# A gated sigmoid on one core: stores of four-row groups and a second load held back

## The chip, the cores and the metric

The kernel runs on one core of a Trainium2 chip. The metric is device time in microseconds for one execution. A smaller number is better. Three runs of the kernel before gave 933.16, 933.18 and 934.11 us; their median is 933.18 us.

## The reference

The input is a matrix of 8192 rows and 8192 columns in float32. The left half of each row is multiplied by the sigmoid of the right half, element by element.

```python
def reference(x):                      # x: (8192, 8192) float32
    a, b = np.split(x, 2, axis=-1)
    return a * (1 / (1 + np.exp(-b)))  # (8192, 4096) float32
```

So 268.4 MB have to be read and 134.2 MB written, and each output element needs one sigmoid and one product.

## The kernel before, in words

SBUF, the on-chip memory, has 128 partitions. A tile is 256 consecutive rows: each partition holds `R = 2` neighbouring rows, which lie in one piece of 64 KiB in HBM. There are 32 tiles. A tile goes through four steps.

- **Load** (`load`, line 46). The SP engine issues one DMA of 128 pieces of 64 KiB into one of two load slots, `x_sb0` and `x_sb1` (line 34). Tile i uses slot i mod 2. The load of tile i waits until the products of tile i - 2 are done, since these read the same slot (line 50).
- **Sigmoid** (line 61). ScalarE (ACT) waits for the tile to land and overwrites the right halves in place. A whole tile is one instruction on 128 x 8192 elements. The first and the last tile are cut into four instructions of 128 x 2048 (`fourths`, line 95).
- **Product** (line 72). VectorE (DVE) multiplies the left halves by the sigmoids and writes the packed result into one of two output buffers, `o_sb0` and `o_sb1`, of 32 KiB a partition (line 35). It waits until the store that last used the buffer has landed, and for the sigmoid. One semaphore for each buffer, `ready`, counts both: a store adds 16, the first sigmoid of a tile adds 1 (lines 62 to 66).
- **Store** (`store`, line 78). ACT's queue issues one DMA of 128 pieces of 32 KiB, which waits for the tile's products. The last tile's store is cut into four DMAs of 128 pieces of 8 KiB, issued from SP's queue.

All orders are written out by hand in `trace` (line 91): each engine takes its instructions in the order in which the loop emits them, and a waiting instruction holds those behind it on its engine. On ACT the order is sigmoid of tile i, store of tile i, sigmoid of tile i + 1. On SP it is one load after the other, then the last stores. The load of tile 0 is moved ahead of the program's start barrier (`_launch_early`). At the end (`close`) GpSimd clears the semaphores, and SP waits for the last stores.

Loads and stores run on the same 16 DMA engines through two queues: q1 is fed by SP, q10 by ACT. In the profile an entry such as "SPq" or "ACTq" is a DMA that the engine issues. Both load slots and both output buffers together take 192 KiB of each partition.

Of the kernel before, what the change touches and what calls it, by code (L numbers as in the profile page):

```python
# [1 line left out]

# [4 lines left out]

P = 128
R = 2
SLOTS = 2  # L10


class _Program:

    def __init__(self, nc, x, out):
        self.nc = nc
        fp32 = mybir.dt.float32
        n_rows, n_cols = x.shape
        self.half = n_cols // 2  # L30
        self.n_tiles = n_rows // (P * R)
        self.x = x.rearrange("(n p r) m -> n p (r m)", p=P, r=R)
        self.out = out.rearrange("(n p r) m -> n p (r m)", p=P, r=R)
        self.xs = [nc.alloc_sbuf_tensor(f"x_sb{s}", [P, R * n_cols], fp32).ap() for s in range(SLOTS)]
        self.os = [nc.alloc_sbuf_tensor(f"o_sb{s}", [P, R * self.half], fp32).ap() for s in range(SLOTS)]
        self.loaded = [nc.alloc_semaphore(f"loaded{s}") for s in range(SLOTS)]
        self.ready = [nc.alloc_semaphore(f"ready{s}") for s in range(SLOTS)]
        self.product = nc.alloc_semaphore("product")
        self.sigmoid = nc.alloc_semaphore("sigmoid")
        self.arrived = nc.alloc_semaphore("arrived")  # L40
        self.last = nc.alloc_semaphore("last")
        self.to_ready = [0] * SLOTS
        self.products = self.sigmoids = self.lasts = 0
        self.done = {}

    def load(self, i, after=None):
        s = i % SLOTS
        ins = self.nc.sync.dma_start(out=self.xs[s][:, :], in_=self.x[i]).then_inc(self.loaded[s], 16)
        if i >= SLOTS:
            ins._wait_ge(self.product, self.done[i - SLOTS])  # L50
        return ins

    def work(self, i, pieces):

        nc, s = self.nc, i % SLOTS
        rows = self.xs[s].rearrange("p (r h m) -> p r h m", r=R, h=2)
        packed = self.os[s].rearrange("p (r m) -> p r m", r=R)
        waits = []
        for k, (r, c) in enumerate(pieces):
            b = rows[:, r, 1, c]  # L60
            sig = nc.scalar.activation(out=b, in_=b, func=mybir.ActivationFunctionType.Sigmoid)  # L61
            if k == 0:
                sig._wait_ge(self.loaded[s], 16 * (i // SLOTS + 1))
                self.to_ready[s] += 1 + (16 if i >= SLOTS else 0)
                waits.append((self.ready[s], self.to_ready[s]))
                sig.then_inc(self.ready[s], 1)
            else:
                self.sigmoids += 1
                waits.append((self.sigmoid, self.sigmoids))
                sig.then_inc(self.sigmoid, 1)  # L70
        for (r, c), wait in zip(pieces, waits):
            mul = nc.vector.tensor_mul(out=packed[:, r, c], in0=rows[:, r, 0, c], in1=rows[:, r, 1, c])  # L72
            mul._wait_ge(*wait)
            mul.then_inc(self.product, 1)
            self.products += 1
        self.done[i] = self.products

    def store(self, i, lo=0, hi=None, products=None):
        s, final = i % SLOTS, i == self.n_tiles - 1
        hi = R * self.half if hi is None else hi  # L80
        queue = self.nc.sync if final else self.nc.scalar
        ins = queue.dma_start(out=self.out[i][:, lo:hi], in_=self.os[s][:, lo:hi])
        ins._wait_ge(self.product, self.done[i] if products is None else products)
        if final:
            self.lasts += 16
            ins.then_inc(self.last, 16)
        else:
            ins.then_inc(self.ready[s], 16)
        return ins

    def trace(self):

        n, half = self.n_tiles, self.half
        whole = [(slice(0, R), slice(0, half))]
        fourths = [(slice(r, r + 1), slice(h * half // 2, (h + 1) * half // 2)) for r in range(R) for h in range(2)]
        self.load(1)
        for i in range(n):
            self.work(i, fourths if i in (0, n - 1) else whole)
            if i + SLOTS < n:
                self.load(i + SLOTS)  # L100
            if i < n - 1:
                self.store(i)
        for k in range(4):
            self.store(n - 1, k * half // 2, (k + 1) * half // 2, self.products - 3 + k)

    def close(self):


        nc, s = self.nc, (self.n_tiles - 2) % SLOTS
        for engine in (nc.scalar, nc.vector, nc.sync):  # L110
            engine.drain().then_inc(self.arrived, 1)  # L111
        nc.gpsimd.wait_ge(self.arrived, 3)
        nc.gpsimd.wait_ge(self.ready[s], self.to_ready[s] + 16)
        ids = sorted(h.num for h in (*self.loaded, *self.ready, self.product, self.sigmoid, self.arrived))
        assert ids == list(range(ids[0], ids[-1] + 1)) and self.last.num not in ids
        nc.gpsimd.sem_clear(range(ids[0], ids[-1] + 1))
        nc.gpsimd.drain()
        nc.sync.wait_ge(self.last, self.lasts).then_inc(self.last, -self.lasts)


def _launch_early(nc):

    SP = mybir.EngineType.SP
    entry, body = (b.instructions for b in nc.main_func.blocks[:2])
    load = next(i for i in body if i.engine == SP and i.opcode == "DMACopy")
    assert not load.sync_info.on_wait
    body.remove(load)
    where = next(k for k, i in enumerate(entry) if i.engine == SP and i.opcode == "Drain")  # L130
    entry.insert(where, load)


@with_exitstack
def kernel(
    ctx: ExitStack,
    tc: tile.TileContext,
    x: bass.AP,
    out: bass.AP,
):  # L140
    nc = tc.nc
    prog = _Program(nc, x, out)
    tc.info.no_tile_sem_insts.add(prog.load(0).ins.name)
    tc.close()
    tc.compile()  # L145
    _launch_early(nc)
    prog.trace()
    prog.close()


# [1 line left out]
_INS = ['x']  # L152
_OUTS = [((8192, 4096), 'float32')]


# [23 lines left out]
```

## Time and profile before

| what | value |
|---|---|
| median of three runs | 933.18 us |
| the profiled execution's own time | 933.08 us |
| its span, first to last instruction | 931.8 us |
| DVE busy, 38 products | 278.6 us |
| ACT busy, 38 sigmoids and a table load | 226.8 us |
| DMA packets, bytes moved | 9649, 402.67 MB |
| mean rate over the span | 432 GB/s |
| DVE waits for ACT | 647.1 us |
| ACT waits for loads | 693.9 us |

Busy times are sums over the span. The span is a little shorter than the execution's time, because something lies before the first and after the last instruction. A wait of a compute engine counts only where it delays the end. The packet count holds the data packets and one small completion packet for each transfer and DMA engine; the latter raises the semaphore by one, so that 16 mean that a transfer has landed.

### The profile page before, as it was taken

How to read it: one execution, taken by the hardware profiler on the slowest of the kernel's cores; microseconds unless marked ns; L12 is line 12 of the kernel's file. 1: busy time of each engine (PE TensorE's matmuls, PEld its weight loads, DVE VectorE, ACT ScalarE, POOL GpSimd, SP SyncE). 2: the span in 40 equal slices, each digit the busy share in tenths (PEclk: the TensorE clock that was granted, in tenths of full speed). 3: DMA queues.
4: the chain of work that ended last, by engine and by line, in shares of the span. 5: the costliest groups of instructions: out<-in, count | busy, mean ns of one | idle time of the engine just before them, and what ended most of it. 6: DMA issues, size and time to landing. Idle time of an engine off the chain costs nothing.

```text
span 931.8 us, 190 instructions
## 1 busy us (share of the span) xinstructions
DVE 278.6 (30%) x38; ACT 226.8 (24%) x39; POOL 0.2 (0%) x4
## 2 busy tenths in 40 slices
DVE  0333213333133331233312333123331233312333
ACT  1323330233311333113331133311333203332033
POOL 0000000000000000000000000000000000000000
DMA  9999999999999999999999999999999999999999
GB/s 405 428 450 428 422 456 405 450 428 428 450 421 435 428 436 442 428 428 450 450 405 430 442 456 428 412 463 408 450 428 428 450 408 447 428 428 450 426 429 405
DMA packets 9649, 402.67 MB, mean 432 GB/s; under 512 B 1072, under 2 KB 1072, under 8 KB 1072
## 3 DMA queue, kind: packets, MB, share of 16 engines
q1 hardware_dynamic: 5184, 272.63, 67.7%
q10 hardware_dynamic: 4464, 130.03, 32.3%
q14 instruction: 1, 0.01, 0.0%
HBM read 268.44 MB, written 134.22 MB: 432 GB/s over the span
## 4 chain that ended last, share of the span: by engine, by line
DMA 73%; DVE 15%; ACT 12%; DVEq 0%; issue 0%
DMA x_sb<-in_x_dram 73%; DVE o_sb L72 15%; ACT x_sb L61 12%; DVEq L111 0%
## 5 line engine op out<-in xcount | busy, mean ns | idle before, releaser
L72 DVE TENSOR_TENSOR o_sb<-x_sb 128x8192 f32<-128x8192 f32 (+1 forms) x38 | 278.6, 7344 | 647.1 <-ACT x_sb L61 647.1
L61 ACT ACTIVATE x_sb<-x_sb 128x8192 f32<-128x8192 f32 (+1 forms) x38 | 225.5, 5949 | 693.9 <-DMA x_sb<-in_x_dram 693.9
L61 ACT ACT_TABLE_LOAD x1 | 1.3, 1283 | 1.4 <-PEq L145 1.4
L163 POOL MEMSET const-bfloat16-1.0<- 128x1 bf16 x1 | 0.1, 102 | 0.0
L163 POOL MEMSET const-uint8-127<- 128x1 uint8 x1 | 0.1, 102 | 0.0
L163 POOL MEMSET const-float32-0.0<- 128x1 f32 x1 | 0.1, 99 | 0.2 <-issue 0.2
L163 POOL MEMSET const-float32-1.0<- 128x1 f32 x1 | 0.1, 99 | 0.0
## 6 DMA issues: line engine op xcount, KB each, us to landing
out_dram<-o_sb ACTq DMA_DIRECT2D x31, 4096.0 KB, 34.8
out_dram<-o_sb SPq DMA_DIRECT2D x4, 1024.0 KB, 5.7
x_sb<-in_x_dram SPq DMA_DIRECT2D x32, 42.2
```

The lines of the kernel that those rows point to most:

```text
L61: sig = nc.scalar.activation(out=b, in_=b, func=mybir.ActivationFunctionType.Sigmoid)
L72: mul = nc.vector.tensor_mul(out=packed[:, r, c], in0=rows[:, r, 0, c], in1=rows[:, r, 1, c])
L163: nc = _bacc.Bacc("TRN2", target_bir_lowering=False, num_devices=1)
```

## The change

Two neighbouring tiles become a group of 512 rows, in which each partition holds four neighbouring rows, 128 KiB in one piece of HBM. A tile is still 64 KiB a partition: tile i is the half i mod 2 of group i div 2. So both the number and the size of the loads stay. In HBM, neighbouring partitions of a load now lie 128 KiB apart instead of 64.

The two output buffers become one of 64 KiB a partition, `o_sb`. The even tile's products fill its first half and the odd tile's its second half, and one store of 128 pieces of 64 KiB writes both, after the odd tile's products. The products of the next even tile wait until the whole store has landed. The SBUF taken is the same.

The loads of even tiles wait as before for the products of the tile that used the slot. The load of an odd tile i + 1 waits on `ready` until the sigmoid of the even tile i has run. `ready` is now a single semaphore: the sigmoid of an even tile adds 32 and a group's store adds 16. For the load the threshold is 16 below the one that the even tile's product waits for, so that the store of the group before need not have landed.

The first tile is cut into two pieces of one row each instead of four. In the last group the even tile is stored by itself with pieces of 32 KiB on ACT's queue, and the odd tile in four quarters as before. GpSimd no longer waits for the last whole-tile store before it clears the semaphores; SP waits for it with the quarters, on `last`.

```diff
-        self.x = x.rearrange("(n p r) m -> n p (r m)", p=P, r=R)
-        self.out = out.rearrange("(n p r) m -> n p (r m)", p=P, r=R)
+        self.x = x.rearrange("(g p r) m -> g p (r m)", p=P, r=2 * R)
+        self.out = out.rearrange("(g p r) m -> g p (r m)", p=P, r=2 * R)
...
-        self.os = [nc.alloc_sbuf_tensor(f"o_sb{s}", [P, R * self.half], fp32).ap() for s in range(SLOTS)]
+        self.os = nc.alloc_sbuf_tensor("o_sb", [P, 2 * self.packed], fp32).ap()
...
-    def load(self, i, after=None):
-        s = i % SLOTS
-        ins = self.nc.sync.dma_start(out=self.xs[s][:, :], in_=self.x[i]).then_inc(self.loaded[s], 16)
-        if i >= SLOTS:
-            ins._wait_ge(self.product, self.done[i - SLOTS])
+    def load(self, i):
+        g, s = divmod(i, 2)
+        part = self.x[g][:, s * self.tile : (s + 1) * self.tile]
+        ins = self.nc.sync.dma_start(out=self.xs[s], in_=part).then_inc(self.loaded[s], 16)
+        if i > 1 and s:
+            ins._wait_ge(self.ready, self.to_ready - 16)
+        elif i > 1:
+            ins._wait_ge(self.product, self.products)
         return ins
...
             if k == 0:
-                sig._wait_ge(self.loaded[s], 16 * (i // SLOTS + 1))
-                self.to_ready[s] += 1 + (16 if i >= SLOTS else 0)
-                waits.append((self.ready[s], self.to_ready[s]))
-                sig.then_inc(self.ready[s], 1)
+                sig._wait_ge(self.loaded[s], 16 * (g + 1))
+            if k == 0 and s == 0:
+                self.to_ready += 32 + (16 if g else 0)
+                waits.append((self.ready, self.to_ready))
+                sig.then_inc(self.ready, 32)
...
-    def store(self, i, lo=0, hi=None, products=None):
-        s, final = i % SLOTS, i == self.n_tiles - 1
-        hi = R * self.half if hi is None else hi
-        queue = self.nc.sync if final else self.nc.scalar
-        ins = queue.dma_start(out=self.out[i][:, lo:hi], in_=self.os[s][:, lo:hi])
-        ins._wait_ge(self.product, self.done[i] if products is None else products)
+    def store(self, g, lo, hi, products, final=False):
+        queue = self.nc.sync if g == self.n_tiles // 2 - 1 and lo else self.nc.scalar
+        ins = queue.dma_start(out=self.out[g][:, lo:hi], in_=self.os[:, lo:hi])
+        ins._wait_ge(self.product, products)
         if final:
             self.lasts += 16
-            ins.then_inc(self.last, 16)
-        else:
-            ins.then_inc(self.ready[s], 16)
-        return ins
+        ins.then_inc(self.last if final else self.ready, 16)
...
         self.load(1)
         for i in range(n):
-            self.work(i, fourths if i in (0, n - 1) else whole)
-            if i + SLOTS < n:
-                self.load(i + SLOTS)
-            if i < n - 1:
-                self.store(i)
-        for k in range(4):
-            self.store(n - 1, k * half // 2, (k + 1) * half // 2, self.products - 3 + k)
+            g, s = divmod(i, 2)
+            self.work(i, by_row if i == 0 else fourths if i == n - 1 else whole)
+            if s == 0 and i > 0:
+                self.load(i + 1)
+            if s == 0 and i < n - 2:
+                self.load(i + 2)
+            if s and i < n - 2:
+                self.store(g, 0, 2 * packed, self.products)
+            elif i == n - 2:
+                self.store(g, 0, packed, self.products, final=True)
+            elif i == n - 1:
+                for k in range(4):
+                    lo = packed + k * half // 2
+                    self.store(g, lo, lo + half // 2, self.products - 3 + k, final=True)
...
-        nc.gpsimd.wait_ge(self.ready[s], self.to_ready[s] + 16)
```

## The prediction

> **What bounds the kernel now.** I read the page's slices first, then its queues and issues, then the instruction groups by shape, the timeline, and last the DMA packets one by one.
>
> ```profile
> span 931.8 us, 190 instructions
> ...
> DVE 278.6 (30%) x38; ACT 226.8 (24%) x39; POOL 0.2 (0%) x4
> ...
> DMA  9999999999999999999999999999999999999999
> ...
> q1 hardware_dynamic: 5184, 272.63, 67.7%
> q10 hardware_dynamic: 4464, 130.03, 32.3%
> ...
> out_dram<-o_sb ACTq DMA_DIRECT2D x31, 4096.0 KB, 34.8
> out_dram<-o_sb SPq DMA_DIRECT2D x4, 1024.0 KB, 5.7
> x_sb<-in_x_dram SPq DMA_DIRECT2D x32, 42.2
> ```
>
> No compute engine passes 30%, the DMA row is 9 in every slice, and the two queues' shares add to 100.0%: all 16 DMA engines work through the whole span. q1 carries loads and the last four stores, q10 the other 31 stores. Only shorter packets can save time, and anything that leaves the DMA engines empty is paid in full. The page's chain, loads 73%, is read accordingly: a load takes 42 us to land because it queues.
>
> ```profile
> L72 DVE TENSOR_TENSOR o_sb<-x_sb 128x8192 f32<-128x8192 f32 x30 | 260.8, 8692 | 608.3 <-ACT x_sb L61 608.3
> L61 ACT ACTIVATE x_sb<-x_sb 128x8192 f32<-128x8192 f32 x30 | 210.9, 7029 | 653.0 <-DMA x_sb<-in_x_dram 653.0
> L72 DVE TENSOR_TENSOR o_sb<-x_sb 128x2048 f32<-128x2048 f32 x8 | 17.8, 2286 | 38.8 <-ACT x_sb L61 38.8
> L61 ACT ACTIVATE x_sb<-x_sb 128x2048 f32<-128x2048 f32 x8 | 14.6, 1898 | 41.0 <-DMA x_sb<-in_x_dram 41.0
> ```
>
> A whole tile costs 7.03 us of sigmoid and 8.69 us of product: 15.7 us, beside 29 us of DMA.
>
> ```profile
> 32.66 57.10 SPq L48 DMA_DIRECT2D x_sb<-in_x_dram  x3
> 32.66 0.38 ACTq L82 DMA_DIRECT2D out_dram<-o_sb  x1
> 44.76 7.03 ACT L61 ACTIVATE x_sb<-x_sb 128x8192 f32<-128x8192 f32 x1 [15.66 <-DMA x_sb<-in_x_dram]
> 51.82 8.69 DVE L72 TENSOR_TENSOR o_sb<-x_sb 128x8192 f32<-128x8192 f32 x1 [19.19 <-ACT x_sb L61]
> 60.55 0.36 ACTq L82 DMA_DIRECT2D out_dram<-o_sb  x1
> ...
> 919.08 6.94 SPq L82 DMA_DIRECT2D out_dram<-o_sb  x4
> ```
>
> From 32.66 us each product releases a load and a store together, so neither queue is empty again before 914 us.
>
> The packet records say the rest. A DMA gives each engine 8 packets and one 4-byte completion packet. A 64 KiB load packet takes 2.418 us, a 32 KiB store packet 1.213, an 8 KiB one 0.309, a completion 0.009. With both queues filled, every engine alternates load and store packets one for one. Loads alone (21 to 33 us) and stores alone (914 to 931 us) keep these durations. The stream runs without a gap from 1.0 us to 931.4 us. The fastest and slowest engine end a transfer 0.5 to 0.7 us apart, and the semaphore follows the slowest by 0.3 to 0.6 us, for a store 0.44 at most.
>
> **The change, part by part.** In what follows E is a group's even tile, O its odd tile.
>
> *Packets.* Thirty 32 KiB-row stores become fifteen 64 KiB-row stores. Per engine 30 x 8 x 1.213 = 291.12 us becomes 15 x 8 packets of 64 KiB. No store of that size is in the trace. Its bounds are two 32 KiB packets (2.426) and the load packet of equal bytes (2.418). I take the load's, whose size it has: 120 x 2.418 = 290.16, so -0.96 us (the other end: 0). Fifteen completions fewer: 15 x 0.009 = -0.14. Loads stay 32 transfers of 128 x 64 KiB.
>
> *First tile in two rows.* Between the shapes' means the sigmoid grows (7029 - 1898) / 6144 = 0.835 ns an element and the product 1.043. Hence 3.61 and 4.42 us for 128x4096. Tile 0 lands at 21.8; two sigmoids and the second product end at 21.8 + 7.2 + 4.4 = 33.4, with starts 33.5. The third load is issued there, while the second has packets until 40.4. Cost nothing, hidden by load 1 with 7 us to spare.
>
> *The cycle.* One group is 24 packets an engine, 8 E, 8 O, 8 store: 58.03 us, if no engine runs dry. I place it from 0 = end of the previous O on the slowest engine, with E queued behind it.
>
> - Semaphore 0.44, sigmoid to 7.50, product to 16.2; store issued. E fills the queue until 19.35. How long until an issued transfer can run? The first load's packets come 1.0 to 1.3 us after issue on idle engines; the last four stores start at most 1.9 us after theirs (919.08, 921.0). So the store is there at 17.2 to 18.1; the fastest engine ends E at 18.65. Margin 0.5 to 1.4 us; it starts at 19.36.
> - E landed at 19.8, sigmoid to 26.85. Only now is O issued (before, the load would have gone out behind the last product, 10 us earlier). The even load behind it on SP is held too, harmless since it waits for a later product anyway. What covers the hold is the store, with the engines to itself until 38.7. The first store of before, issued at 32.66 beside loads, saw two whole load packets end before its own began; packet boundaries up to 3.26 us after issue still went to the other queue. By that row O starts at the boundary after 26.88 + 3.26 = 30.1, at 31.45, behind five store packets. The remaining three store packets alternate with O and the store ends at 19.36 + 11 x 2.418 = 45.96.
> - The product of E waits for that, since the output buffer is single. ACT queues nothing behind it but the sigmoid of O, not yet landed. Semaphore to 46.4, product to 55.1, the next even load available 56.2 to 57.1. O's last packet ends at 58.05, on the fastest engine 57.35. Margin 0.25 to 1.2 us: thin, but positive, so the next group starts in phase. Cost nothing.
>
> [...]
>
> *Tail.* The last product of E frees a 32 KiB-row store of 9.7 us behind the last O. The four quarters of O come 4.2 us after its landing and then every 2.2 us. DMA work left after O is 9.7 + 4 x 2.48 = 19.6 us, and the last quarter is available about 12.7 us after O's end: covered. Before and after end on the same quarter store.
>
> **Sum.** The profiled execution took 933.08 us: span 931.77 and 1.31 around it; the median shown, 933.18, is 0.10 above. 933.08 - 0.96 - 0.14 = **932.0 us**, 0.12% less. A measurement of this kernel can tell about 0.2%, 1.87 us, from no change: this is "same".
>
> **Rivals.**
>
> *Restarts cost (slower).* When the first store woke the empty q10 amid loads, the load packet before it took 3.23 to 3.47 us instead of 2.418 on all engines: 0.92 us in the mean with nothing moved. That happened once, since no queue ran empty again. After, the store queue starts from empty 16 times (15 more) and the load queue 15 times. If each store start costs 0.92: 932.0 + 13.8 = 945.8; if load starts do too: 959.6. Against: q1 ran empty at 914 and woke at 921.0 with no extra time; an instruction fetch on a third queue at 761.6 added 0.24 us beyond its own packet, on one engine. So 0.92 may be the price of a queue's first use. I cost a further restart at 0, the row of the warm queue; bounds 0 and 0.92, or 0.24 (30 x 0.24 = 7.2: 939.2). It decides at (1.87 + 1.10) / 30 = 0.1 us a restart.
>
> *The even load comes late (slower).* If O wakes faster, at 29.03, after four store packets, the store ends at 48.4, and the product and issue reach the engines 1.2 to 2.1 us after the fastest have run dry. Some 1.5 us for each of 15 groups: 954. The row for it is the last stores' 1.9 us; against it the 3.26 above. Even with five packets, half a microsecond beyond the thin margins, once a group, gives 939.5. A store's landing signal 1.56 us later than the 0.44 of the rows would do as much and more, 938 to 952, and I give it 0.03 of the chances below. [...]
>
> *The first restart's price goes too (faster).* If the first store finds only E's last packet, its 0.92 may vanish beside the packet savings: 931.06, just past 0.2%.
>
> *Memory rows.* Partition steps double in HBM, loads 64 to 128 KiB, stores 32 to 64 KiB; every packet could lengthen. The trace shows both old steps at full rate, nothing on the new ones. A 1% longer load packet would give 938.2. [...]
>
> **How the numbers follow.** No stall, 932.0 (931.3 to 935.0): 0.50. Faster, about 931.06: 0.08. Small bubbles (0.24 a restart, half a microsecond a group, a later landing signal with its 0.03, slower rows with 0.02), 935 to 942: 0.17. Store restarts at full price, about 946: 0.12. Both restarts, or the late even load, 950 to 960: 0.13. So faster 0.08, same 0.50, slower 0.42. The range leaves out the last case, the lower part of the fast one and the upper half of the 946 case, together 0.2: 931.0 to 946.5. The likeliest case alone spans 931.3 to 935.0.
>
> **What would show it.** Right: DMA shares still adding to 100%, 64 KiB store packets of 2.418 us, a store landing 30 us after its issue (16.25 to 46.4), an even load 23 us (55.2 to 58.05 + 19.8), an odd one 32 us (26.9 to 58.5), the product of E waiting for the store and not the sigmoid, groups every 58.0 us. Wrong: groups longer than 58.03; load or store packets above 2.43 where a queue starts (restarts); a gap before each even load (late load); all packets longer (memory rows).

## The result and the profile after

The changed kernel takes 961.85 us (median of five runs, 959.98 to 963.74) against 933.2 us before (median of five, 933.16 to 934.11). The ratio is 1.0302, 95% interval 1.029 to 1.0314: about 28.7 us slower. The profiled execution is the one of 961.85 us; its span is 960.5 us against 931.8.

These are the lines of the changed kernel's page that answer to the first fence of the prediction: the span, the compute engines, the DMA engines' busy tenths in 40 slices, the queues (packets, MB, share of 16 engines' span) and the issues (count, KB each, median us from issue to landing).

```profile
span 960.5 us, 186 instructions
...
DVE 278.4 (29%) x36; ACT 226.6 (24%) x37; POOL 0.2 (0%) x4
...
DMA  9999999999999989999999999999999899999999
...
q1 hardware_dynamic: 5184, 272.63, 67.1%
q10 hardware_dynamic: 2304, 130.02, 31.8%
...
out_dram<-o_sb ACTq DMA_DIRECT2D x1, 4096.0 KB, 13.7
out_dram<-o_sb SPq DMA_DIRECT2D x4, 1024.0 KB, 8.6
x_sb<-in_x_dram SPq DMA_DIRECT2D x32, 28.2
out_dram<-o_sb ACTq DMA_DIRECT2D x15, 33.1
```

The compute engines did the same work. The two queue shares show the loss in two parts. They add to 98.9%, where before they added to 100.0%: 0.011 x 960.5 = 10.6 us in which a DMA engine had no packet. And the packets themselves take 0.989 x 960.5 = 949.9 us of engine time, 18 us more than the 931.8 before, although there are fewer of them.

Two lines of the waits and a stretch of the timeline show where. The waits have the waiting engine and line, what it waited for, the total in us, how often, and the longest.

```profile
DVE o_sb L81 <- DMA out_dram<-o_sb: 498.7, 15, 34.2
DVE o_sb L81 <- ACT x_sb L69: 174.4, 17, 26.9
```

```profile
57.06 0.38 ACTq L90 DMA_DIRECT2D out_dram<-o_sb  x1
60.92 7.03 ACT L69 ACTIVATE x_sb<-x_sb 128x8192 f32<-128x8192 f32 x1 [12.62 <-DMA x_sb<-in_x_dram]
67.98 31.59 SPq L53 DMA_DIRECT2D x_sb<-in_x_dram  x2
90.53 8.69 DVE L81 TENSOR_TENSOR o_sb<-x_sb 128x8192 f32<-128x8192 f32 x1 [33.50 <-DMA out_dram<-o_sb]
100.19 7.03 ACT L69 ACTIVATE x_sb<-x_sb 128x8192 f32<-128x8192 f32 x1 [32.24 <-DMA x_sb<-in_x_dram]
```

Every even tile's product waits for the group's store, as forecast. But it starts at 90.53 us and ends at 99.2, and only then is the next even load issued (the second of the two SP issues). The odd load has landed by 100.2 and nothing else is queued. The packet records of one DMA engine over the same stretch, start times in us, say why (E is a group's even tile, O its odd tile, S the store):

```
last load packet of E   57.18, 2.85 us long (2.418 is usual)
store packets           60.04 (3.12 us long)  63.15  65.57  67.98  70.39
O and store alternate   O 72.81  S 75.25  O 77.66  S 80.08  O 82.49  S 84.91
                        O 87.32                  the 8th and last store packet ended at 87.32
store's completion      89.73                    its own turn, after one more load packet
O alone                 89.74  92.15  94.57  96.98, ends 99.40
next even load          101.19                   issued 99.2
```

A packet is called long here when it takes more than the usual time of its size, 2.418 us for 64 KiB and 1.213 for 32 KiB; what is added up is the excess. From the packet records of all 16 engines, in the mean per engine: 10.1 us more than before without a packet; 5.3 us of long first packets of even loads behind such a gap; 14.4 us of long packets where a store starts (last load packet 8.9, first store packet 5.5), of which 0.9 stood in the kernel before; 0.3 us where an odd load starts; and 1.1 us saved by fewer packets. -1.1 + 10.1 + 5.3 + 13.5 + 0.3 = 28.1 of the 28.7 us. Eight of the even loads come late; each leaves the engines empty for 0.2 to 2.3 us in the mean and has a first packet that is 0.6 to 0.7 us too long, about 1.9 us together.

So two things had to be explained: the even loads that come late, and the price of a store's start.

### The profile page after: what moved, and what is told of

It reads as the page before. It is cut to its first block, busy times and chain, and to the rows that moved or that the text cites. A ratio compares the mean times of both kernels' runs of the same rounds, so it can differ in the third digit from the quotient of the medians.

```text
span 960.5 us, 186 instructions
## 1 busy us (share of the span) xinstructions
DVE 278.4 (29%) x36; ACT 226.6 (24%) x37; POOL 0.2 (0%) x4
## 4 chain that ended last, share of the span: by engine, by line
DMA 73%; DVE 14%; ACT 12%; DVEq 0%; issue 0%; ACTq 0%
DMA x_sb<-in_x_dram 48%; DMA out_dram<-o_sb 24%; DVE o_sb L81 14%; ACT x_sb L69 12%; DVEq L124 0%; ACT L69 0%; ACTq L69 0%
## 5 line engine op out<-in xcount | busy, mean ns | idle before, releaser
L81 DVE TENSOR_TENSOR o_sb<-x_sb 128x8192 f32<-128x8192 f32 (+2 forms) x36 | 278.4, 7743 | 673.1 <-DMA out_dram<-o_sb 498.7
L69 ACT ACTIVATE x_sb<-x_sb 128x8192 f32<-128x8192 f32 (+2 forms) x36 | 225.3, 6269 | 699.4 <-DMA x_sb<-in_x_dram 699.4
```

Of the source, the lines that this page charges most:

```text
L81: mul = nc.vector.tensor_mul(out=packed[:, r0:r1, c0:c1], in0=rows[:, r0:r1, 0, c0:c1], in1=rows[:, r0:r1, 1, c0:c1])
```

## Experiments

### The late even load: the hold made longer, shorter, and left out

The odd load is held 1.9 us longer by a sigmoid on a spare buffer:

```diff
         if i > 1 and s:
-            ins._wait_ge(self.ready, self.to_ready - 16)
+            ins._wait_ge(self.hold, self.holds)
...
+        if s == 0 and i > 0:
+            extra = nc.scalar.activation(
+                out=self.spare, in_=self.spare, func=mybir.ActivationFunctionType.Sigmoid
+            )
+            extra.then_inc(self.hold, 1)
+            self.holds += 1
```

> The changed kernel with the odd load held 1.9 us longer: ScalarE runs one more sigmoid of 128x2048 on a spare buffer behind the even tile's, and the odd load waits for that. Stores, their 64 KiB packets and their starts from an empty queue stay. Theory: one store packet more runs unshared, so the store ends about 2.4 us earlier and the even load is in time: no engine runs dry, about 15 us less than the changed kernel. What is left are the starts of the store queue. If these cost 0.90 us each with 64 KiB packets, 946.5 us. If their price in the changed kernel was partly the disorder that late even loads leave (halved stores paid only 0.3 us a start), 936 to 938 us. Rival, the gaps have another cause than the store's end: 960 us or more.

Measured: 950.95 us, ratio to before 1.0192 (1.0166 to 1.0218), 10.9 us less than the changed kernel. The lines of its page, from an execution of 952.17 us:

```profile
span 950.9 us, 202 instructions
...
q1 hardware_dynamic: 5184, 272.63, 67.1%
q10 hardware_dynamic: 2304, 130.02, 32.7%
```

The shares add to 99.8%: 1.9 us without a packet instead of 10.6. In the first group the store now has six packets ahead of the odd load instead of five, and its completion comes at 87.39 us on the same engine instead of 89.73. What is left, 949.0 us of packet time, are long packets: 12.3 us at the starts of stores, 3.4 us at even loads that come just in time. The store starts cost about what the theory gave them, 12.3 / 15 = 0.8 us each; "936 to 938" is out.

The hold shortened by 3.4 us, with even tiles worked row by row:

```diff
-            self.work(i, by_row if i == 0 else fourths if i == n - 1 else whole)
+            self.work(i, by_row if s == 0 else fourths if i == n - 1 else whole)
```

> The changed kernel with every even tile worked row by row (two sigmoids of 3.61 us and two products of 4.42), so that the odd load goes out after the first row's sigmoid, 3.4 us earlier. Theory: the odd load takes every second turn of the DMA engines one or two packets earlier, the store ends 2.4 to 4.8 us later, and the even load as much: 15 x 2.4 to 15 x 4.8 us on top of the changed kernel, 998 to 1034 us. Rival, the moment of the odd load does not matter to the gaps: 962 us.

Measured: 994.89 us (1.064 to 1.0682 of before). The store issues come 58.6 and 65.7 us apart in turn, so the loss is a full one in every second group alone, 3 us below the range. The moment of the odd load sets the gap.

No hold at all:

```diff
-        if i > 1 and s:
-            ins._wait_ge(self.ready, self.to_ready - 16)
-        elif i > 1:
+        if i > 1:
             ins._wait_ge(self.product, self.products)
...
-            if s == 0 and i > 0:
-                self.load(i + 1)
-            if s == 0 and i < n - 2:
+            if i < n - 2:
                 self.load(i + 2)
```

> The changed kernel without the hold: an odd load waits for the products of the odd tile before it, as in the kernel before, and goes out with the group's store. Theory: it queues behind the even load and alternates with the store from the start, so that both end together, 58 us into the group; semaphore, product and issue of the next even load, 10 to 11 us, then stand open in every group, and its slow first packet: 933.2 - 1.1 + 15 x (0.9 + 10.5 + 0.6) = 1112 us, between 1090 and 1130. Rival, the hold itself is what leaves the engines dry: 933 to 947 us.

Measured: 1042.0 us. The direction holds and the size is missed: store issues come about 60.7 and 68.0 us apart in turn, so here too only about every second group has its gap of 8 to 9 us, and the even loads between are late by about 1 us; I had charged the full gap to each. The page:

```profile
DMA  9999599997999969999799996999979999799987
...
q1 hardware_dynamic: 5184, 272.63, 63.4%
q10 hardware_dynamic: 2304, 130.02, 28.9%
```

7.7% of 1040.8 us, 80 us, is without a packet, in nine of the forty slices. The hold is what keeps this design usable; it was a little too short.

### The price of a store's start: queues

One line sends the changed kernel's stores to SP's queue:

```diff
-        queue = self.nc.sync if g == self.n_tiles // 2 - 1 and lo else self.nc.scalar
+        queue = self.nc.sync
```

> The changed kernel with one line different: the group stores go to SP's queue, behind the loads, instead of ACT's. Theory: the 28.7 us are two costs, 14.4 us of long packets where the store queue starts from empty beside loads (0.90 us each) and about 15 us of engines run dry before an even load, with its slow first packet. With one queue neither can occur: no queue ever starts from empty, and the store runs unshared, so it ends at 38.7 instead of 45 to 48 us of a group and the even load is issued about 10 us before it is needed. Expected 933.2 - 1.1 (fewer packets) - 0.9 (the one restart of the kernel before) = 931.2 us, between 930.7 and 931.8, with no long packet after the first load. Rival 1, the long packets belong to the turn from loads to stores and not to a queue's start: 16 turns at 0.9 stay, 946 us. Rival 2, the wider step between rows in HBM or the 64 KiB store packets are slow: over 940 us, with long packets anywhere.

Measured: 943.12 us, 1.0105 of before (1.009 to 1.012). Neither 931 nor 946.

```profile
span 941.2 us, 186 instructions
...
q1 hardware_dynamic: 7488, 402.66, 99.7%
```

No even load is late (the issue of even loads comes some 10 us before it is needed), and in the second to fifth stretch of 58 us the turn from load to store costs 0.03 to 0.13 us of long packets, all seams together. So the turn itself is not the price. From the seventh on 0.4 to 0.8 us a stretch come back, mostly where the store ends and the odd load begins, and 2.0 us in the sixteenth, where the last group's stores begin. At the same time the engines drift apart: the first and the last of them ended a transfer 0.6 us apart at first and 2 to 3 us apart later, and at the end of the run the engines stand idle for 2.5 us in the mean, waiting for the last one.

The kernel before with one queue:

```diff
-        queue = self.nc.sync if final else self.nc.scalar
+        queue = self.nc.sync
```

> The kernel before with its stores on SP's queue instead of ACT's, nothing else. Theory: its only restart, 0.92 us at 36 us, goes: 932.3 us, all packets at 2.418 and 1.213. Rival, the turn from loads to stores costs: 31 turns at 0.9 us give 961 us. Rival, the 0.92 us is the price of a first store and not of a queue: 933.2 us with the long packet still there.

Measured: 939.01 us, 1.0057 of before (1.0044 to 1.007): slower, not faster. The long packets at the first store are still there (1.1 us), so the 0.92 us of the kernel before belonged to the first store and not to a queue that starts from empty, and the prediction's row for a restart was the wrong row. (In the grouped kernels with one queue the first store cost 0.4 us.) The rest of the loss is drift: the engines' ends move from 0.7 to 4.8 us apart and 3.3 us stand idle at the end.

The changed kernel's queues exchanged, loads on ACT's and stores on SP's:

```diff
+        if i > 1 and s:
+            self.nc.scalar.wait_ge(self.product, self.products - 1)
-        ins = self.nc.sync.dma_start(out=self.xs[s], in_=part).then_inc(self.loaded[s], 16)
+        ins = (self.nc.scalar if i > 1 else self.nc.sync).dma_start(out=self.xs[s], in_=part).then_inc(self.loaded[s], 16)
...
-        queue = self.nc.sync if g == self.n_tiles // 2 - 1 and lo else self.nc.scalar
+        queue = self.nc.sync
```

> The changed kernel with the queues exchanged: loads from tile 2 on go to ACT's queue, stores to SP's; the order and the waits stay (ScalarE also waits for the odd product before it issues an odd load, which is long done by then). Theory, the long packets come with the start of a store beside loads, whichever queue carries it: about 962 us, the long packets still at the last load packet and the first store packet. Rival, ACT's queue itself is slow to start: the long packets move to the starts of the loads.

Measured: 962.78 us, as the theory had it. Long packets stay at the starts of stores (13.1 us: last load packet 9.0, first store packet 4.1) and of late even loads (6.0). Which queue carries what made no difference here.

One queue, and no hold:

```diff
+            if i > 1:
+                ins._wait_ge(self.product, self.products)
...
             if s and i < n - 2:
                 self.store(g, 0, 2 * packed, self.products)
+                self.load(i + 2)
```

(The two waits of `load` become this one, and the issue of the odd load at the even tile goes.)

> The changed kernel with all stores on SP's queue and the odd load issued right behind the group's store, without the hold. With one queue nothing alternates, so the hold has no work to do; without it a store and a load always lie in the queue. In the one-queue kernel with the hold, 8 us of long packets came where the store ends and a load begins that was issued only 7 to 10 us before. Theory, late issue makes them: they go, and with them most of the 2.5 us by which the engines end apart: 931 to 934 us. Rival, each turn between load and store pieces of 64 KiB disturbs engines that are out of step: about 942 us again.

Measured: 942.78 us, 1.0096 of before (1.0079 to 1.0113), with 8.4 us of long packets as with the hold, and 2.4 us idle at the end. The late issue of the odd load does not make them; the rival's figure came true.

### The price of a store's start: size, start, lateness

Each group's store as two DMAs with 32 KiB pieces, each half with a semaphore of its own, so that the even product waits for the first half alone:

```diff
+            elif k == 0:
+                self.to_ready1 += 1 + (16 if g else 0)
+                waits.append((self.ready1, self.to_ready1))
+                sig.then_inc(self.ready1, 1)
...
-        ins.then_inc(self.last if final else self.ready, 16)
+        ins.then_inc(self.last if final else self.ready1 if lo else self.ready, 16)
...
-                self.store(g, 0, 2 * packed, self.products)
+                self.store(g, 0, packed, self.products)
+                self.store(g, packed, 2 * packed, self.products)
```

> The changed kernel with each group's store cut into its even and its odd tile, two DMAs of 32 KiB pieces issued one behind the other, each half with its own semaphore. So the product of the even tile waits for 8 short packets only and runs some 15 us earlier; the hold and the restart of the store queue stay. Theory: the gaps before the even loads go and the restarts stay: 933.2 + 15 x 0.90 = 946.7 us, between 944 and 949. Rival 1, one cause, the late even load makes the long packets as well: 933 us. Rival 2, the 64 KiB store packets make them: 933 us too, with no long packet.

Measured: 938.49 us, 1.0052 of before (1.0039 to 1.0066), between the two forecasts. The line that answers to the changed kernel's first wait line is this:

```profile
DVE o_sb L86 <- DMA out_dram<-o_sb: 203.4, 15, 14.6
```

The product waits 14.6 us at most instead of 34.2, and no engine runs dry. But the store starts cost only 4.4 us in all, 0.3 each, of which the kernel's first store has 0.9.

The same two halves, with the even product waiting for both:

```diff
-                self.to_ready += 32 + (16 if g else 0)
+                self.to_ready += 48 + (32 if g else 0)
...
-                self.store(g, 0, 2 * packed, self.products)
+                self.store(g, 0, packed, self.products)
+                self.store(g, packed, 2 * packed, self.products)
```

> The changed kernel with each group's store issued as two DMAs of 32 KiB pieces, one behind the other, and the next even product waiting for both, so that against the changed kernel only the packet size differs, and against the halved stores with their own semaphores only the wait. The total says little: sixteen short packets that alternate with 64 KiB loads end later, about 53 to 56 us into the group, and the even load comes 5 to 10 us late in every or every second group: 990 to 1090 us. What counts are the long packets at the start of a store (last load packet, first store packet). If the price of a start goes with the packet size, about 5 us in all, as with the separate semaphores; if it goes with the late even load and the disorder it leaves, 14 us, as in the changed kernel.

Measured: 1016.6 us in one run, and 12.4 us of long packets at the starts of stores (last load packet 10.8, first store packet 1.7), 14 us being the forecast for "not the size". The price does not go with the packet size alone: behind late even loads the last load packet is 0.7 to 0.9 us long here, in the changed kernel about 1.1. It comes down, with pieces of the same size, when the even load is in the queue long before.

Whether an empty queue's start costs anything was tried on the kernel before with one queue, by moving part of each store to ACT's queue. First 16 of the 128 partitions:

```diff
+        parts = [(self.nc.sync, 0, P)] if final else [(self.nc.sync, 0, P - 16), (self.nc.scalar, P - 16, P)]
```

> The kernel before with stores on SP's queue, but 16 of the 128 partitions of each whole store on ACT's queue, issued together: one packet for each DMA engine, so that ACT's queue starts from empty once a tile beside busy engines, 31 times, and bytes and data packets stay the same. Theory, the start of the empty store queue itself has the price, whatever its size: 932.3 + 31 x 0.9 = 960 us. Rival, the price belongs to the first large store after a stretch of loads alone: about 932.5 us.

Measured: 1083.54 us. It doesn't answer the question. With 16 partitions the packets of 32 KiB on ACT's queue took up to 6.8 us instead of 1.213, and the engines came up to 33 us apart: the cut itself slows the engines. Why it does, no run here shows.

Then the last 2 KiB of all 128 partitions' 32 KiB, and in another kernel the last 16 KiB (4096 in place of 512):

```diff
+        cut = hi - 512
+        parts = [(self.nc.sync, lo, hi)] if final else [(self.nc.sync, lo, cut), (self.nc.scalar, cut, hi)]
```

> The kernel before with its stores on SP's queue, but the last 2 KiB of each partition's 32 KiB on ACT's queue, issued together, so that an otherwise empty queue starts once a tile, 31 times, with 8 small packets an engine. [...] More packets cost 31 x (8 x 0.008 + 0.009) = 2.3 us on top of the 939.0 us of the one-queue kernel: 941 us if a start costs nothing. At 0.3 us a start 951, at 0.9 us 969 us.

> The same with half of each partition's store, 16 KiB, on ACT's queue: the same number of starts, packets of 16 KiB. 941 us if a start costs nothing, 951 at 0.3 us, 969 at 0.9 us. If the price grows with the packet, it is above that of the 2 KiB kernel.

Measured: 940.61 and 940.76 us against the 941 for a free start. In the second, long packets add to 2.6 us beside the first load's, 1.0 of them at the first store, and drop to under 0.1 us in 58 us from the eighth such stretch on, the last apart. Beside a filled load queue, a queue's start from empty cost nothing by itself in these two.

And whole stores of every second tile on ACT's queue:

```diff
-        queue = self.nc.sync if final else self.nc.scalar
+        queue = self.nc.sync if final or s == 0 else self.nc.scalar
```

> The kernel before with the whole stores of even tiles on SP's queue and those of odd tiles on ACT's, so that ACT's queue starts from empty 15 times with a whole store, 32 KiB packets, while SP's queue still has loads. If a whole store's start beside a filled load queue costs 0.9 us, 939.0 + 13.8 = 952.8 us. If the price is due only where the loads run out as the store starts, 939 to 941 us, as with the partial stores of 2 and 16 KiB.

Measured: 943.73 and 959.72 us in two runs, so the total decides nothing. The profile belongs to the first: 15 stores start on ACT's queue, and the long packets next to them add to 0.7 us. So a whole store's start beside a filled load queue was free here too. The time went into drift: engines up to 17 us apart, 6.5 us idle in the last two groups.

Last, the halved stores with their own semaphores, and the odd tiles in quarters, so that the store is issued earlier:

```diff
-            self.work(i, by_row if i == 0 else fourths if i == n - 1 else whole)
+            self.work(i, by_row if i == 0 else fourths if s else whole)
```

> The halved stores with their own semaphores, and every odd tile worked in quarters, so that its products end 11.1 us after its landing instead of 15.8 and the group's store is issued 4.6 us earlier, with three load packets still to run instead of one. Theory, the long first packets (4 to 5 us in all, 938.5 us) are the time by which the store's issue comes too late for the engines: they go, 934 to 935 us. Rival, the price belongs to the hand-over from one queue to the other whenever it comes: 938 us or more.

Measured: 934.95 us, 1.0015 of before (1.0006 to 1.0025), the best of the grouped kernels. The timeline around the second group's store, first of the halved stores, then of this one (start, length, what, and the idle time before):

```profile
116.11 3.76 ACTq L95 DMA_DIRECT2D out_dram<-o_sb  x2
119.97 7.03 ACT L70 ACTIVATE x_sb<-x_sb 128x8192 f32<-128x8192 f32 x1 [12.62 <-DMA x_sb<-in_x_dram]
```

```profile
111.20 0.82 ACTq L95 DMA_DIRECT2D out_dram<-o_sb  x2
122.21 7.03 ACT L70 ACTIVATE x_sb<-x_sb 128x8192 f32<-128x8192 f32 x1 [14.57 <-DMA x_sb<-in_x_dram]
```

In the first, the even tile has landed 3.9 us after the store's issue, its last load packet ending 2.6 to 3.1 us after it, and the first store packet is long on 13 of 16 engines, by up to 0.73 us. In the second, the even load is still running when the store joins it 5.1 to 5.7 us after its issue, and no packet at that start is long. Long packets are left at the kernel's first store (1.1 us), as in the kernel before, and 0.6 us elsewhere; the page's shares add to 100.0%:

```profile
q1 hardware_dynamic: 5184, 272.63, 67.7%
q10 hardware_dynamic: 4464, 130.03, 32.3%
```

For stores that start as the loads run out, lateness is the price. In the halved stores, from the third group on, the first packet begins 2.5 to 2.9 us after the store's issue in the mean of the 16 engines, and is 0.06 to 0.55 us too long. The shorter that lead, the longer the packet: the two add to 3.0 or 3.1 us in every group. In the changed kernel's third group the sum is 3.4 us in the mean (on one engine the packet begins at 179.60 and is 0.66 too long; issue 176.75). The earlier issue itself was tried with the halved stores alone, not with the changed kernel's 64 KiB stores.

## Why the prediction was wrong

**The bound, and what is saved: right.** The kernel is bound by its DMA engines, and what leaves them empty was paid: the 10.1 us without a packet stand in the sum of 28.1 above. Packets of 64 KiB take 2.418 us in the median, of stores and of loads. Nothing is long all over, so the wider steps in HBM cost nothing. The landing signal stayed where the rows had it: the store's completion ends on the slowest engine at 90.05, the product starts at 90.53. No run shows the 1.56 us by which a landing signal comes later in the prediction's second rival: from the end of a store's last completion packet to its semaphore, the stores on ACT's queue took 0.29 to 0.44 us in the kernel before and 0.29 to 0.45 in the changed one.

**The first tile: a miss without a price.** The third load was issued at 35.7, not 33.5, because ScalarE's table load of 1.28 us now came behind the first tile's landing, at 21.99 instead of 1.45. The second load's last packet ended after 40 us.

**"The store ends at 45.96", "Margin 0.25 to 1.2 us", "Cost nothing": the step that failed.** The data packets did end as counted: O behind five store packets, 11 packets from the store's start to its last. But I took the completion packet to follow the last data packet at once. It takes a turn of its own in the alternation, one load packet of 2.418 us later (87.32 and 89.73 in the listing). Then the next even load can run 58.6 to 59.5 us into the group, where O ends at 57.35 to 58.05. The trace of the kernel before had the row already: in all 480 cases, 30 stores on 16 engines, in which loads lay beside a store, its completion came behind one more load packet (on one engine the first store's last data packet ends at 63.00, its completion runs at 65.41). In the listing, from 72.81 to 89.73, the engine turns to the other queue after each 64 KiB piece, and once more for the completion.

The same turn explains why only every second group loses. Behind a late even load the store joins while its last packet still runs, so the load's completion waits behind the first store packet (124.27 after 121.86 on that engine). The odd load goes out that much later, finds six store packets ahead of it, and the next even load is in time again. The store issues come about 58.9 and 60.7 us apart in turn, up to the tenth group. Gaps and slow first packets make 15.4 us together, against the 22 us of my rival, which had the right consequence by the wrong route: O did not wake faster.

**"I cost a further restart at 0, the row of the warm queue": wrong in effect.** Store starts cost 13.5 us, almost the 13.8 of the rival, but not for its reason. The start of an empty queue showed no price beside a filled load queue (940.61 and 940.76 us with 2 and 16 KiB, 0.7 us of long packets in 15 starts with every second store), and the 0.92 us row was the first store's price, which the kernel before pays with one queue too. What I had costed at nothing beside it was the margin of "0.5 to 1.4 us" for the store's issue: a store issued that shortly before the loads run out comes too late, and issuing it 4.9 us earlier removes the price where it was tried, with the halved stores. The rows for it, 1.0 to 1.9 us from issue to first packet, were those of the first load and of the 8 KiB stores; beside running loads the halved stores take 3.0 us. By an estimate from that figure the store is there at 16.2 + 3.0 = 19.2 us, where E ends at 18.65 to 19.35: a margin of -0.6 to 0.1 us. Of the 14.4 us at store starts this accounts for nine of the sixteen, those behind an even load that was in time or 0.2 us late, with 6.6 us, the first store's 1.0 among them. The other 7.8 us are not covered by it.

**The cases.** I had "store restarts at full price" and "the late even load" as alternatives, at 0.12 and within 0.13. Both happened at once: 932.0 + 13.5 + 15.4 = 960.9, against 961.85.

**What stays open.** The 7.8 us lie at the seven stores behind an even load that came at least 0.8 us late. There the store is issued 4.1 to 4.8 us ahead, and still the last load packet is long by about 1.1 us. In the kernel without hold, where every even load from the third on is late, the stores are issued 4.4 to 5.3 us ahead and each pays 1.0 to 1.2 us on the load packet before it. So lateness covers the stores whose even load was in time, not these. Nor is its sum of 3 us fixed: in two groups of the longer hold the store begins 1.3 and 1.5 us after its issue and is only 0.5 and 0.8 us too long. The kernels that pay all have even loads that come late or at the last moment, and where loads wait in the queue from far ahead such starts were free or cheap; whether that is the cause was not tried by itself.

## What to carry to other kernels

Where all DMA engines are busy through the whole span, count turns and not bytes alone: here a store beside loads was complete when its completion packet had had its turn, one load packet of 2.418 us later, and a margin of 0.25 to 1.2 us, counted without that turn, was none. Issue a transfer early enough before the queue beside it runs out: some 5 us, two packets, were enough with the halved stores, though not behind late even loads. And keep a load queue filled from far ahead rather than timing it with a hold: the kernel before does that, and none of the regrouped versions beat it (the best took 1.0015 of its time).

## What was not expected of the hardware

- One queue is worse than two for the same packets: 939.01 against 933.84 us. With two filled queues that alternate, the 16 engines end within 0.5 to 0.73 us of each other through all 31 tiles; with one queue they drift to 4.8 us apart, and the last engine sets the end.
- The kernel's first store costs 0.9 us of long packets in the kernel before and 1.1 with one queue, where no queue starts from empty.
- A store over 16 partitions beside one over 112 took the kernel to 1083.54 us with the same bytes and data packets.
